# Gates copied out of PSUM by ScalarE, and a state-space branch that is issued later, in a two-layer hybrid attention kernel

## The chip, the cores and the metric

The kernel runs on one core of a Trainium2 chip. Its engines are TensorE (PE in the rows, its weight loads PEld), VectorE (DVE), ScalarE (ACT), GpSimd (POOL) and SyncE (SP, which here only issues transfers). Time is device microseconds (us) of one execution; the number that counts is the median of the runs.

## The reference

Two layers; each normalises x (1024 tokens by 1024 features), makes one wide projection, and feeds three mixers whose outputs are multiplied by SiLU gates and go through one output projection.

```
h = rms_norm(x, norm_g[l]);  proj = h @ w_in[l]
(qa, ka, va, iq, ik, iw, ga, u, gb, cq, ckv, kpe, gc) = split(proj)
ya = dsa_branch(...)     # A: an indexer scores all keys, the top 256 of each query are attended to
yb = s5_branch(u, ...)   # B: complex diagonal state space, scan over time, GELU, GLU
yc = mla_branch(...)     # C: latent attention
mixed = concat(ya * silu(ga), yb * silu(gb), yc * silu(gc))
x = x + mixed @ w_out[l]
```

All is float32. Of branch B three parts count here: a static part (tables and small matrices from the parameters alone), the states (inputs times a matrix, then a complex scan over 128 steps of 8 tokens), and the outputs (states times a matrix, GELU, GLU).

## The kernel before, in words

**Matmuls.** A float32 product is made of three reduced-precision ones (`mm3`, L163 to L165): high by high, low by high, and high by the low part of the weights. So a block of weights is loaded (`raw`), its high part `whi` is written by ACT (L150) and its low part `wlo` by POOL or DVE (L151). PE can't start a block before `whi`, and can't do its third product before `wlo`.

**Stages of a layer.** First the narrow projections and the indexer; then the indexer's scores (PE L927, ACT `rl` L928, DVE sums L933); then the selection of the top keys on DVE (search, then marks L1028 to L1031, whose last instruction writes `bias`, one 128-query block after another; a branch L1040 follows it for a rare case). While DVE selects, PE makes the steps written in `STEPS = "L5C6Q7U01234"`: three projections L, C, Q, the eight gates 0 to 7 of 128 features each, and U, the inputs of branch B. Then the attention items run, block 7 of branch A first: its scores (PE L1394 and L1395), their masked maximum on DVE (L1210, which needs `bias`), exponentials on ACT (L1218), transposes of the exponentials on PE (L1238). Then the output projection.

**Gates.** `gates(c)` makes two halves of 512 tokens, 24 matmuls each, into a PSUM bank `gt`. ACT writes th = tanh(gt/2) (L1164), and DVE writes gate = (th+1)*gt (L1165), reading `th` and the bank. The bank comes free when both have read it. `th` lies in a ring of five 2 KB pieces that other work shares (`s5bd`, `s5rho`, `gl` and more). The gate goes to DRAM and is read back late.

**PSUM** has eight banks: six in one ring (tag `s`: gates, scores, branch B's sums), two for transposes (tag `tr`).

**Branch B** is a generator that the code steps along on a clock of its own: each matmul group of the main line adds its ticks, and each `yield d` of branch B says after how many ticks (times `S5M` = 1.5) it goes on. `static` makes tables (POOL and DVE products L276), small transposed matrices (PE L421 and L438, copied by ACT as `s5k` L423 and `s5w` L439) and rotors `s5R` on POOL (L261 to L266). `chunks` makes the states: sums `vr`, `vi` on PE, products and scans on DVE (L475 to L486), rotation back on POOL (`s5x`, L276). Its last `yield ST2` sets how long after that the `outputs` are written: PE L504 to L506, GELU on ACT and DVE (L509 to L513), transposes L520. It is done for two halves of the groups, 0 and 1. The layer's parameters are prepared by another generator, `params`.

**Order.** A scheduler gives each engine its instructions as one list, worked out before the run, from what each needs and a priority that grows along the program. `side(gen, delay, behind)` starts such a generator after `delay` ticks; `behind` is added to the priority of everything that it issues. In the run each engine goes through its list in order, and waits where the next instruction's inputs, bank or page are not ready.

Of the kernel before, what the change touches and what calls it, by code (L numbers as in the profile page):

```python
# [14 lines left out]
AF = mybir.ActivationFunctionType  # L15
ALU = mybir.AluOpType
# [26 lines left out]
K2 = 5  # L43
MIXT = 4.0
MIX4 = 32
S5P = 0
KVP = -400
TH = (0, 0, 0, 0, 0, 0, 4, 4)
STEPS = "L5C6Q7U01234"
S5W = (0, 0)  # L50
S5M = 1.5
FT = 0.6
ST2 = 8.0
ST3 = 4.0
GLP = 0
KTP = (0, 0, 0)
# [30 lines left out]
def hybrid_kernel(ctx, tc, A, out, dbg=None, layers=DEPTH):  # L87
    nc = tc.nc
    V, S, G, T = nc.vector, nc.scalar, nc.gpsimd, nc.tensor
# [9 lines left out]
    def page(shape, dt, name):  # L99
        return pg.tile(shape, dt, tag="pg", name=name)  # L100
# [4 lines left out]
    def ps_s(shape, name="s"):  # L105
        return pp.tile(shape, F32, tag="s", name=name, bufs=BANKS)
# [12 lines left out]
    def scr(shape, dt, name):  # L119

        n = int(np.prod(shape[1:])) * (2 if dt == BF16 else 4)
        if n > 2048:
            return page(shape, dt, name)
        tag, bufs = ("k1", K1) if n <= 1024 else ("k2", K2)
        return sm.tile(shape, dt, tag=tag, name=name, bufs=bufs)
# [254 lines left out]
    def s5(l, Z, us, yb):  # L380
# [77 lines left out]
        def chunks(gh):  # L458
# [4 lines left out]
            for i in range(4):  # L463
                for e in range(2):
                    rs = slice(64 * e, 64 * e + 64)
                    for x, d in ((0, vr), (1, vi)):
# [24 lines left out]
                                  RR[:, :, j0], RI[:, :, j0], xa[:, :, j0], xb[:, :, j0])  # L491
            yield ST2

# [72 lines left out]
    def side(gen, delay=0.0, behind=0):  # L566

        sides.append([gen, clock[0] + delay, behind])
# [127 lines left out]
    for t in range(8):  # L696
# [3 lines left out]
        if t == 3:  # L700
# [3 lines left out]
            params = s5_params()  # L704
# [10 lines left out]
    for l in range(layers):  # L715
# [16 lines left out]
        def proj_halves(evac):  # L732
            w = [ws.get(), ws.get()]
            for hf in range(2):
                if hf:
                    for _ in turn_h(1, hT, htok, g_in):
                        pass
                pss = [ps_s([128, 2, 256], "pj") for _ in range(2)]
                for kh in range(2):
                    hi, lo, n = w[kh]  # L740
                    for p in range(2):
                        proj_step(pss[p], 4 * hf + 2 * p, kh, hi, lo, n)
                        if kh == 1:
                            evac(2 * hf + p, pss[p])
# [387 lines left out]
        def channels():  # L1132

            hi, lo, _ = ws.get()
            for hf in range(2):
                cs = slice(512 * hf, 512 * hf + 512)
                ps = ps_s([128, 512], "gt")
                for k in range(8):
                    mm3(ps, hi[:, k, :], lo[:, k, :], h_hi[k][:, cs], h_lo[k][:, cs], k == 0, k == 7)
                    tick(0.64)  # L1140
                yield hf, cs, ps
# [18 lines left out]
        def gates(c):  # L1160
            g = page([128, 1024], F32, f"gate{c}")
            for hf, cs, ps in channels():
                th = scr([128, 512], F32, "th")
                S.activation(th, ps, AF.Tanh, scale=0.5)  # L1164
                V.scalar_tensor_tensor(g[:, cs], th, 1.0, ps, op0=ALU.add, op1=ALU.mult)  # L1165
            nc.sync.dma_start(gate_d[c], g)

        yb = []
# [2 lines left out]
        def tables_then_s5():  # L1171
            yield from s5_tables(l, Z)
            for d in s5(l, Z, us, yb):
                yield S5M * d
            for o in range(2):
                gate_in(3 + o)
                (G if GLP else V).tensor_tensor(mixf[3 + o], yb[o], mixf[3 + o], op=ALU.mult)
                mixed.add(3 + o)
        if l == 0:
            side(params, 1.0)  # L1180
        proj_halves(ev_g2)
        proj(ev_iq, tps=range(1, 4), outer="I" not in INNER)

# [279 lines left out]
        def at(i):  # L1463
            if i == S5AT:
                side(tables_then_s5(), behind=S5P)
            if i == CQAT:
# [5 lines left out]
        for i, x in enumerate(STEPS, 8 - len(STEPS)):  # L1472
            at(i)
            if i in QAT:
                next(its)
            if x.isdigit():
                gates(int(x))
            elif x == "U":
                inputs_s5()
            else:  # L1480
                proj(dict(L=ev_g4, C=ev_g3, Q=ev_g5)[x], outer=x not in INNER)
# [56 lines left out]
        for hf in range(2):  # L1538
            cs = slice(512 * hf, 512 * hf + 512)
# [4 lines left out]
        for g in range(2):  # L1544
# [9 lines left out]
            for t in range(8):  # L1554
                cs = slice(128 * t, 128 * t + 128)
                ps = ps_s([128, 512], "po")
# [87 lines left out]
```

## Time and profile before

| | before |
|---|---|
| median of 3 runs | 1354.73 us (1354.72 to 1354.92) |
| profiled execution | 1345.04 us, of which the span shown in the trace is 1343.3 us |
| mean granted TensorE clock over the span | 0.967 of 2.4 GHz |
| PE busy | 1254.7 us, 93% |
| DVE, ACT, POOL busy | 907.3, 662.5, 680.8 us |

The profile is of one execution, 9.7 us shorter than the median of the timed runs; differences are worked out in it and then taken from the median. An engine that is 93% busy need not lose only the other 7%: it is also slower wherever its granted clock falls.

### The profile page before, as it was taken

To read this page: it belongs to the slowest core of one execution; us is meant where nothing else is said; L and a number is where in the kernel's file an instruction comes from. 1 tells how busy PE (TensorE), PEld (TensorE's weight loads), DVE (VectorE), ACT (ScalarE), POOL (GpSimd) and SP (SyncE) were. 2 spreads that over 40 slices of the span, in tenths; PEclk is the share of its full clock that TensorE was granted. 3 is DMA by queue.
4 is the path that set the end of the run, shared out by engine and by line. 5 is a ranking of instruction groups with operands and counts; after the bars stand their busy time and mean duration, and the time that the engine had idled before them with its cause. 6 is when DMAs were issued, how large, how long until landed. Compare 5 with 4: busy or idle time off the path is not lost. (4 is left out here: it accounts for less than half of the span.)

```text
span 1343.3 us, 23872 instructions
## 1 busy us (share of the span) xinstructions
PE 1254.7 (93%) x8644; PEld 1065.8 (79%) x8644; DVE 907.3 (68%) x2430; ACT 662.5 (49%) x1505; POOL 680.8 (51%) x1109
## 2 busy tenths in 40 slices
PE   4898999978999999999999989998889999999998
PEld 4896998757788778877899878977668786887787
DVE  5758889974786797741253878999566778775121
ACT  4346831121778777751243666112148786877300
POOL 3889259766431456312347953795770335553210
PEclk9998999888999999999999989999879999999999
DMA  7200241332110100241140013222303010004202
GB/s 219 72 2 28 83 127 59 96 96 91 39 62 17 42 27 8 76 175 41 79 130 29 20 60 111 82 88 81 121 19 94 8 58 17 12 32 159 78 32 94
DMA packets 78490, 92.78 MB, mean 69 GB/s; under 512 B 13536, under 2 KB 61280, under 8 KB 78368
## 3 DMA queue, kind: packets, MB, share of 16 engines
q1 hardware_dynamic: 77216, 87.03, 20.1%
q0 software_dynamic: 1152, 4.19, 1.0%
q8 instruction: 68, 1.11, 0.3%
q14 instruction: 54, 0.44, 0.1%
HBM read 63.53 MB, written 26.50 MB: 67 GB/s over the span
## 5 line engine op out<-in xcount | busy, mean ns | idle before, releaser
L753 PE MATMUL pj<-whi,hh 128*128 128x256 f32 (+1 forms) x608 | 173.5, 286 | 0.0
L756 PE MATMUL pj<-whi,hl 128*128 128x256 f32 (+1 forms) x608 | 172.3, 285 | 0.0
L755 PE MATMUL pj<-wlo,hh 128*128 128x256 f32 (+1 forms) x608 | 172.1, 283 | 0.0
L151 POOL TENSOR_TENSOR wlo<-raw,whi 128x1024 fp32r<-128x1024 f32 (+1 forms) x40 | 94.3, 2372 | 129.1 <-ACT whi L150 116.5
L163 PE MATMUL gt<-hh,whi 128*128 128x512 f32 x320 | 132.2, 413 | 10.4 <-DVE gate L1165 10.4
L165 PE MATMUL gt<-hh,wlo 128*128 128x512 f32 x320 | 130.7, 409 | 4.1 <-POOL wlo L151 4.1
L164 PE MATMUL gt<-hl,whi 128*128 128x512 f32 x320 | 130.3, 407 | 0.0
L753 PEld LDWEIGHTS pj<-whi,hh 128*128 128x128 f32 x608 | 117.9, 194 | 1.1 <-issue 0.2
L755 PEld LDWEIGHTS pj<-wlo,hh 128*128 128x128 f32 x608 | 117.7, 194 | 0.8
L756 PEld LDWEIGHTS pj<-whi,hl 128*128 128x128 f32 x608 | 117.2, 193 | 0.3
L1244 ACT ACTIVATE pt<-s 128x512 f32<-128x512 f32 (+1 forms) x154 | 82.9, 555 | 47.5 <-PE s L1238 38.2
L933 DVE SCALAR_TENSOR_TENSOR acc<-rl,iw,acc 128x384 f32<-128x384 f32 (+5 forms) x84 | 94.0, 1120 | 13.7 <-ACT rl L928 10.9
L163 PE MATMUL po<-whi,mix 128*128 128x512 f32 x256 | 98.5, 392 | 1.6 <-DVE gin L1261 1.6
L164 PE MATMUL po<-wlo,mix 128*128 128x512 f32 x256 | 99.8, 391 | 0.0
L165 PE MATMUL po<-whi,mix 128*128 128x512 f32 x256 | 99.5, 389 | 0.0
L150 ACT ACTIVATE whi<-raw 128x1024 fp32r<-128x1024 f32 (+1 forms) x54 | 55.9, 1055 | 85.3 <-DMA qa_d<-qo 30.6
L1238 PE MATMUL s<-ident,P 128*128 128x128 f32 x588 | 93.1, 277 | 1.5 <-ACT pt L1244 0.7
L1561 DVE TENSOR_TENSOR xn<-xn,po 128x512 f32<-128x512 f32 x32 | 22.0, 687 | 103.3 <-PE po L165 103.2
L1218 ACT ACTIVATE P<-P,nb,qsc 128x1024 f32<-128x1024 f32 (+7 forms) x96 | 82.4, 864 | 17.0 <-DVE nb L1216 17.0
L1218 ACT ACTIVATE P<-P,nb,asum 128x1024 f32<-128x1024 f32 (+7 forms) x96 | 82.6, 866 | 12.5 <-DVE nb L1216 11.8
L928 ACT ACTIVATE rl<-s 128x512 f32<-128x512 f32 (+3 forms) x160 | 74.0, 540 | 24.4 <-PE s L927 16.6
L1208 DVE TENSOR_SCALAR_CACHE_REDUCE P<-s 128x512 f32<-128x512 f32 (+3 forms) x144 | 74.2, 548 | 16.5 <-PE s L1372 9.9
(453 smaller groups left out, 3625.3 us busy)
## 6 DMA issues: line engine op xcount, KB each, us to landing
raw<-in_w_in SPq DMA_DIRECT2D x32, 512.0 KB, 4.9
gate_d<-gate SPq DMA_DIRECT2D x16, 512.0 KB, 2.9
gin<-gate_d SPq DMA_DIRECT2D x16, 512.0 KB, 4.4
raw<-in_w_out SPq DMA_DIRECT2D x16, 512.0 KB, 6.9
x<-in_x SPq DMA_DIRECT2D x8, 512.0 KB, 4.9
cq_d<-cqs SPq DMA_DIRECT2D x16, 256.0 KB, 2.1
cqT<-cq_d POOLq DMA_DIRECT2D x8, 512.0 KB, 6.0
xn<-in_x SPq DMA_DIRECT2D x8, 512.0 KB, 10.1
```

The lines of the kernel that those rows point to most:

```text
L151: (eng or G).tensor_tensor(lo, raw, f(hi), op=ALU.subtract)
L163: T.matmul(ps, lh, rh, start=start, stop=False)
L164: T.matmul(ps, lh, rl, start=False, stop=False)
L165: T.matmul(ps, ll, rh, start=False, stop=stop)
L753: T.matmul(o, hk, hi[:, k, 0:n], start=kh == 0 and i == 0 and k == 0, stop=False, skip_group_check=True)
L755: T.matmul(o, hk, lo[:, k, 0:n], start=False, stop=False, skip_group_check=True)
L756: T.matmul(o, lk, hi[:, k, 0:n], start=False, stop=kh == 1 and k == 3, skip_group_check=True)
L933: V.scalar_tensor_tensor(a, r[:, 0:nk], w, a, op0=ALU.mult, op1=ALU.add, **({"accum_out": ssum[:, b - 2:b - 1]} if h == 7 else {}))
L1208: V.tensor_scalar(Ps[j][:, c0:c1], p[:, 0:c1 - c0], 1.0, -3.0e38, op0=ALU.mult, op1=ALU.max, accum_out=m)
L1218: S.activation(Ps[j][:, 0:nk], Ps[j][:, 0:nk], AF.Exp, bias=nb[:, j:j + 1], scale=it["scale"][:, j:j + 1], accum_out=sums[:, j:j + 1])
L1238: T.transpose(p[:, i, :], Ps[j][:, 128 * kt:128 * kt + 128], ident)
L1244: S.activation(pt[:, 0:n, :], p[:, 0:n, :], AF.Copy)
```

## The change

Four edits. (1) ACT also copies the bank of a gate into the gate's own page, right after its tanh in the program, and DVE's product then reads `th` and that page, both in SBUF; 32 more ACT instructions of 128 by 512 in all, and a bank of a gate is read by ACT alone. (2) Branch B's whole chain is issued with 700 added to its priority (`S5P`). (3) `ST2` goes from 8 to 24, so its outputs are written 36 ticks after its states and not 12. (4) In layer 0 the parameters of branch B start 12 ticks later and not 1.

```diff
-S5P = 0
+S5P = 700
-ST2 = 8.0
+ST2 = 24.0
@@ gates(c)
                 S.activation(th, ps, AF.Tanh, scale=0.5)
-                V.scalar_tensor_tensor(g[:, cs], th, 1.0, ps, op0=ALU.add, op1=ALU.mult)
+                S.activation(g[:, cs], ps, AF.Copy)
+                V.scalar_tensor_tensor(g[:, cs], th, 1.0, g[:, cs], op0=ALU.add, op1=ALU.mult)
@@
         if l == 0:
-            side(params, 1.0)
+            side(params, 12.0)
```

The lines of the changed kernel behind L1164 have numbers higher by one: L1165 is the copy, L1166 the product, L1211 the masked maximum. What the four edits do to the lists of the engines is alike in both layers; the rows are of layer 0.

On DVE, at the end of the selection, the list before is this (`tkw` is a working copy of a block's scores, `m` eight found values of it, `bias` the mask that the last block's marks become; the rare case behind the branch is left out):

```order
L1029 COPY_PREDICATED m_3187<-kp,consts 128x8
L1030 MATCH_REPLACE tkw<-m_3187,tkw 128x1024
L1031 TENSOR_SCALAR bias<-tkw 128x1024
L1040 COMPARE_AND_BRANCH
...
L1165 SCALAR_TENSOR_TENSOR gate_3156<-th,gt 128x512 x2
L1165 SCALAR_TENSOR_TENSOR gate_3251<-th,gt 128x512 x2
L475 TENSOR_TENSOR s5tab<-vr,s5R 128x512
```

In the list of the changed kernel the first of the two gates (the one numbered 3156 before, 3164 now) stands ahead of the last mark:

```order
L1028 MAX m_3195<-tkw 128x8
L1166 SCALAR_TENSOR_TENSOR gate_3164<-th,gate_3164 128x512 x2
L1029 COPY_PREDICATED m_3195<-kp,consts 128x8
L1030 MATCH_REPLACE tkw<-m_3195,tkw 128x1024
L1031 TENSOR_SCALAR bias<-tkw 128x1024
L1040 COMPARE_AND_BRANCH
...
L1166 SCALAR_TENSOR_TENSOR gate_3261<-th,gate_3261 128x512 x2
L475 TENSOR_TENSOR s5tab<-vr,s5R 128x512
```

Two products have moved ahead of the mark and the branch, and none of them reads a bank any more.

On PE, where the gates end and the attention begins, the list before goes from the last gate matmul over four score pairs (`ka_hi`, `ka_lo` are the two parts of the keys) to branch B's outputs (`s5m`, `s5o` are its small matrices), 24 rows of L504 to L506 in all:

```order
L165 MATMUL gt<-hh_222,wlo 128x512
L504 MATMUL s<-s5m,s5U 128x8x16
L1394 MATMUL s<-ka_hi,qA 128x512
L1395 MATMUL s<-ka_lo,qA 128x512
...
L504 MATMUL s<-s5m,s5U 128x8x16
L505 MATMUL s<-s5o,s5x 128x8x16 x2
L506 MATMUL s<-s5o,s5x 128x8x16
L504 MATMUL s<-s5m,s5U 128x8x16
```

In the changed kernel all twelve score pairs of the first three items stand ahead of the outputs, of which 12 rows come there and the other 12 among the later attention work:

```order
L1395 MATMUL s<-ka_hi,qA 128x512
L1396 MATMUL s<-ka_lo,qA 128x512
L504 MATMUL s<-s5m,s5U 128x8x16
L505 MATMUL s<-s5o,s5x 128x8x16
L1395 MATMUL s<-ka_hi,qA 128x512
L1396 MATMUL s<-ka_lo,qA 128x512
L506 MATMUL s<-s5o,s5x 128x8x16
L504 MATMUL s<-s5m,s5U 128x8x16
...
L506 MATMUL s<-s5o,s5x 128x8x16
L1239 MATMUL tr<-ident,P 128x128
```

So the scores went ahead, half of the outputs and their eight transposes went behind the first transposes of the exponentials. The second half of branch B goes much further back, from the first quarter of the attention to its middle. DVE's list follows: its twelve maxima L1210 stood behind the GELU L510 to L513 of the outputs, and now stand right behind the scan L486.

On ACT, the tanh, copies and weight parts of the gates before, and the copies `s5k`, `s5w` of branch B between them:

```order
L1164 ACTIVATE th<-gt 128x512
L150 ACTIVATE whi<-raw 128x1024
L1164 ACTIVATE th<-gt 128x512
L423 ACTIVATE s5k<-tr 16x512 x2
L1164 ACTIVATE th<-gt 128x512
L439 ACTIVATE s5w<-tr 128x512
L1164 ACTIVATE th<-gt 128x512
L439 ACTIVATE s5w<-tr 128x512
```

The same stretch of the changed kernel:

```order
L150 ACTIVATE whi<-raw 128x1024
L1164 ACTIVATE th<-gt 128x512 x2
L423 ACTIVATE s5k<-tr 16x512
L1165 ACTIVATE gate_2996<-gt 128x512 x2
L423 ACTIVATE s5k<-tr 16x512
L439 ACTIVATE s5w<-tr 128x512
L1164 ACTIVATE th<-gt 128x512 x2
L473 ACTIVATE s5rho<-zp 128x512
L439 ACTIVATE s5w<-tr 128x512
L150 ACTIVATE whi<-raw 128x1024
L1165 ACTIVATE gate_3164<-gt 128x512 x2
```

The copies don't always follow their tanh: here they stand behind branch B's copies, and so behind what those wait for.

## Rows read from the trace of the kernel before

**Rows 1.** The page, busy time, share of the span and instructions by engine.

```profile
PE 1254.7 (93%) x8644; PEld 1065.8 (79%) x8644; DVE 907.3 (68%) x2430; ACT 662.5 (49%) x1505; POOL 680.8 (51%) x1109
```

**Rows 2.** Stretches: length, busy PE, PEld, DVE, ACT, POOL (instructions), clock, DMA.

```profile
258.90:343.10 84.20, 70.48 (x321) 55.81 (x321) 56.03 (x105) 21.60 (x35) 52.52 (x105) 0.84 0.26 85
913.60:996.90 83.30, 68.50 (x323) 53.94 (x321) 55.47 (x103) 21.37 (x34) 52.36 (x107) 0.86 0.26 86
```

**Rows 3.** Waits of PE in layer 0's stretch: total us, times, longest.

```profile
PE gt L163 <- DVE gate L1165: 4.4, 1, 4.4
PE pb L1035 <- ACT s5w L439: 3.4, 1, 3.4
PE s L506 <- POOL s5x L276: 3.4, 1, 3.4
```

**Rows 4.** Waits of PE in layer 1's stretch, the longest.

```profile
PE gt L163 <- DVE gate L1165: 5.9, 1, 5.9
```

**Rows 5.** Timeline of DVE, layer 0: start, duration, instruction, idle before and its releaser.

```profile
288.27 2.06 DVE L1031 TENSOR_SCALAR bias<-tkw 128x1024 bf16<-128x1024 f32 x1
291.28 2.48 DVE L1165 SCALAR_TENSOR_TENSOR gate<-th,gt 128x512 f32<-128x512 f32 x4 [0.96 <-DVEq L1040]
...
329.41 0.60 DVE L510 TENSOR_SCALAR gl<-gl 128x512 f32<-128x512 f32 x1 [12.02 <-ACT gl L509]
...
332.11 0.68 DVE L1210 CUSTOM_DVE_ANT_0 P<-s,bias 128x512 f32<-128x512 f32 x1
...
344.00 0.69 DVE L1210 CUSTOM_DVE_ANT_0 P<-s,bias 128x512 f32<-128x512 f32 x1
```

**Rows 6.** Branch B's outputs on PE: half 0 of layer 0, then half 1.

```profile
322.40:334.30 11.90, 11.90 (x41) 8.98 (x41) 4.09 (x10) 1.23 (x2) 7.75 (x17) 0.51 0.08 23
412.20:416.40 4.20, 4.20 (x27) 3.23 (x25) 2.58 (x11) 2.67 (x7) 1.30 (x1) 1.00 0.00 0
```

**Rows 7.** Groups of instructions: count, busy us, mean ns, idle before.

```profile
L1165 DVE SCALAR_TENSOR_TENSOR gate<-th,gt 128x512 f32<-128x512 f32 x32 | 21.0, 682 | 8.1 <-ACT th L1164 5.3 <-DVEq L1040 1.8 <-DMA qa_d<-qo 0.7
L1244 ACT ACTIVATE pt<-s 128x512 f32<-128x512 f32 (+1 forms) x154 | 82.9, 555 | 47.5 <-PE s L1238 38.2 <-PE acc_o L1231 7.7 <-PE s L1395 0.5
```

**Rows 8.** Timeline, products of two SBUF operands on DVE, and of POOL beside the first.

```profile
254.66 3.85 DVE L276 TENSOR_TENSOR s5tab<-zp 128x512 f32<-128x512 f32 x2
254.04 3.92 POOL L1011 TENSOR_TENSOR tkw<-acc,tkm 128x640 f32<-128x640 f32 x2
305.26 0.69 DVE L478 TENSOR_TENSOR s5z<-s5tab 128x512 f32<-128x512 f32 x1
```

**Rows 9.** Timeline of PE: gate matmuls ahead of the stretch, first transposes of exponentials.

```profile
258.02 0.39 PE L163 MATMUL gt<-hh,whi 128*128 128x512 f32 x1
258.25 0.39 PE L164 MATMUL gt<-hl,whi 128*128 128x512 f32 x1
...
343.09 0.66 PE L1238 MATMUL tr<-ident,P 128*128 128x128 f32 x4 [1.19 <-ACT s5gT L521]
```

**Rows 10.** Timeline of ACT and POOL: weight parts for gates, then `s5x`.

```profile
265.36 1.06 ACT L150 ACTIVATE whi<-raw 128x1024 fp32r<-128x1024 f32 x1 [3.27 <-issue]
266.55 2.40 POOL L151 TENSOR_TENSOR wlo<-raw,whi 128x1024 fp32r<-128x1024 f32 x1 [6.68 <-ACT whi L150]
291.23 1.06 ACT L150 ACTIVATE whi<-raw 128x1024 fp32r<-128x1024 f32 x1 [7.01 <-DVEq L1040]
321.09 1.26 POOL L276 TENSOR_TENSOR s5x<-s5tab 128x508 f32<-128x508 f32 x1
```

**Rows 11.** The attention of layer 0 in 20 us stretches, their sum; one stretch of the selection.

```profile
sum 260.00, PE 251.49 PEld 206.43 DVE 190.34 ACT 197.20 POOL 100.90; mean PE 19.35 PEld 15.88 DVE 14.64 ACT 15.17 POOL 7.76
240.00:260.00 20.00, 17.18 (x70) 13.26 (x68) 19.59 (x29) 1.06 (x1) 18.56 (x19) 0.91 0.27 79
```

**Rows 12.** Waits of PE over the whole span, earlier stages.

```profile
PE s L927 <- ACT rl L928: 8.0, 7, 3.9
PE tr L678 <- DVE hl L682: 6.0, 2, 4.5
```

## The prediction

> **What bounds the kernel now.** I read the page first: PE is busy for 93% of the span and no other engine for more than 68% [rows 1]. So time can be gained where PE waits or runs at the lower clock, and of those places I looked at the ones that the change touches. The view by stretches shows them: from the end of the first gates to the first transposes of exponentials, 84.2 us in layer 0 and 83.3 in layer 1, PE is busy 70.5 and 68.5 us at a granted clock of 0.84 and 0.86 [rows 2]. That is 13.7 and 14.8 us of idle time, and 0.16 x 84.2 = 13.5 and 0.14 x 83.3 = 11.7 us lost to the clock: 27.2 and 26.5 us, the most that any edit of this stretch alone can give. In the attention behind it PE is busy 251.5 of 260 us, at full clock [rows 11].
>
> The waits say who is late. In layer 0: 4.4 us for DVE's gate product, 3.4 for the copy `s5w`, 3.4 for `s5x` [rows 3]; in layer 1 the gate's wait is 5.9 [rows 4]. The timeline of DVE explains the first: the last mark runs from 288.27 to 290.33, then comes the branch, and only then, at 291.28, four gate products that PE's banks had waited for [rows 5]. Behind the gates DVE stands still for 12.0 us (GELU, waiting for branch B's outputs) while score banks are ready, since its maxima L1210 are in line behind the GELU; the first starts at 332.11 and the twelfth at 344.00 [rows 5]. PE meanwhile does branch B's outputs at half clock: 41 instructions in 11.9 us at 0.51 [rows 6].
>
> **The change, part by part.**
>
> *ACT copies.* Nothing in the rows is this instruction; the nearest is ACT's copy of a 128x512 PSUM tile, 0.555 us [rows 7]. 32 of them are 17.8 us, 16 to a layer, on an engine that is busy 21.6 of 84.2 us in the stretch [rows 2]; its room hides them, except where one stands behind something late. Without that cover each would hold its bank 0.56 us longer.
>
> *DVE product.* From bank and `th` it takes 0.682 us [rows 7]. A product of two SBUF operands of the same size takes 0.69 [rows 8], so I price the new form the same. The other bound is in the same rows: two such products took 3.85 us together while POOL ran 3.92 us of large tiles beside them, 1.9 each [rows 8]. The Trainium skill (Perfetto Trace Analysis, Optimizing Scalar/DVE Operations) has an access overhead of about 125 ns for DVE on PSUM and 60 on SBUF, by which 32 products would save an estimated 2.1 us of DVE; the two rows at 0.68 and 0.69 don't show that. The same section says that GpSimd and DVE share an SBUF port, and the 1.9 us rows agree.
>
> *Waits for gate banks* (4.4 and 5.9) go, since no bank waits for DVE. What is late next is the weights, so the gain is not the wait. I followed PE through layer 0. The gate matmuls come 0.23 us apart [rows 9]. PE stands at 258.5; it now makes 16 more, to 262.2, and a few of branch B's small matrices, which I estimate at 1.2 us. The next block needs a `whi` that ends at 266.4, and its third products a `wlo` that ends at 268.95 [rows 10]; both hang on earlier transfers that the change leaves. So some 5 us of waiting are new there. 44 matmuls from 269 last 10.1 us, up to 1.7 more at the lower clock: 279 to 281. Then 1.2 us of small matrices, and a wait for four ACT copies in line (two `s5k`, two gate halves, at 0.56 each [rows 7] 2.2 us): the 3.4 us for `s5w` are only moved. `s5w` and the sums `vr`, `vi` with a short wait of their own, some 3 us, end at about 286.5. Two gates, 96 matmuls, are 22 us, with 1 to 3 us (an estimate) for gate copies that stand behind `vi` and for one more `wlo`: 310 to 312.
>
> *Outputs and scores.* The twelve score pairs are next, paced by twelve maxima of 0.68 us [rows 5], 8.2 us, with the scan and a product or two between: 320 to 325. That is 20 us ahead of before, but PE's next instruction, L506, needs the second `s5x`. It ended at 322.35 [rows 10], and now follows two more POOL products in line: about 325. Twelve output rows, 24 instructions, are 24 x 4.2/27 = 3.7 us at full clock, or 24 x 11.9/41 = 7.0 at the half rate seen [rows 6]. So the first transposes of exponentials come between 327 and 337; I take 331, the lower middle, because PE is fed by the scores until just before. Before they came at 343.1 [rows 9]: 12 us earlier. But 3.7 us of outputs and eight transposes (four are 0.66 us [rows 9], so 1.3) now lie behind, in an attention in which PE is full [rows 11], so their 5.0 us come back. Net 7, bounds 11 and 1; if the scores ran at half clock too, so that the transposes came at 341, -3. Layer 1 has the same lists; its longer gate wait (5.9) is swallowed by the same weights, and I give it the same 7.
>
> *The second half of branch B*, moved to the middle of the attention, has the same instructions. PE has no hole there to lose, and DVE is busy 190 of 260 us [rows 11]: cost 0, bounds -3 and +3 per layer.
>
> *Earlier stages.* PE waits 8.0 us in seven places for ACT's `rl` [rows 12]; pages now come free in another order, and ACT's extra copies stand between some `rl`: 0, bounds -3 and +3 per layer. The late parameters thin DVE's list where layer 0's wait for `hl` is, 4.5 of the 6.0 us [rows 12]: 1 us gained, bounds 0 and 4.5.
>
> Sum: 7 + 7 + 0 + 1 = 15 us. The profiled execution would go from 1345.0 to 1330; it stands 9.7 us under the median, and I take the difference from the median: 1354.7 - 15 = 1340.
>
> **The rivals.**
>
> *The stretch flows.* If ACT's copies keep the banks moving, PE's gaps stay short and the half-clock stretch of the outputs goes too. Of 27 us per layer [rows 2], the new waits for weights (5) and for `s5k` and `s5w` (3), without clock loss, would be left, and the 5 us of moved work: 27 - 8 - 5 = 14 per layer, 28 in all, with the prologue 29: 1326. For it: the outputs' half clock followed waits that DVE's order made. Against: the weights' gaps are of the same size as those before which the clock fell.
>
> *It doesn't do what it says.* PE is off DVE, but on ACT, which goes through its list in order, with copies behind branch B's copies and `vi`. If these hold the banks as long as DVE did, and `s5x` and the clock hold the outputs at 337 or later, the 6 us gained are the 5 given back: 1 us per layer, 1352 to 1355. For it: every stall of [rows 3] has a successor in my working.
>
> *Slower, through DVE's operands.* Gate products now read SBUF twice, while in the selection POOL is busy 18.6 of 20 us and DVE 19.6 [rows 11]. If the eight products ahead of the last mark all took 1.9 us for 0.68 [rows 8], that is 9.8 us, and the two that are now in line ahead of the mark are 1.4: the mark would end not at 290.3 but at 301.5. The `whi` of the last gate waits for the branch behind the mark; it began at 291.23 before [rows 10], would begin at 302.4, and the two weight parts take 1.06 and 2.40: 305.9. PE comes to the last gate 48 matmuls before 310 to 312, so at 299 to 301. So up to some 5 us of delay cost nothing, and from there each counts once: here 5 to 6 us, with 3 more at the lower clock, against the 7; with the second half of branch B at its bound, 3, that is a loss of 5 per layer and, less the 1 us of the early stage, 1364. The last mark's delay is the shared port's price in this kernel, whose rule is the one named above. Against it: POOL's large tiles are there for some of the products only, and the rows show 0.69 where it rests.
>
> **How the numbers follow.** Forecast (gain of 4 to 25 us, by the bounds 1 and 11 of a layer, those of the earlier stages, and a share of the clock): 0.57. Flows: 0.13. No change: 0.13. Slower: 0.17, as the moved work and DVE's operands both have unknown prices. A measurement of this kernel tells 0.2%, 2.7 us, from no change. Faster is then 0.57 + 0.13 = 0.70, same 0.13, slower 0.17. The forecast's own range is 1330 to 1351. The range for 8 in 10 takes in most of the flowing case and the near part of the slower one: 1320 to 1359.
>
> **What would show it.** Right: no wait of a gate matmul on DVE; waits of about 3 us and 2.5 for `whi` and `wlo` behind 262; the first L1211 at 312 to 316 and the twelfth by 326; first transposes near 331; a gain that stands at 12 us there and shrinks by about 5 through the attention. Wrong: gate products over 1 us on DVE and a last mark behind 298; a half-clock stretch of 10 us or more still at the outputs or at the scores; a gain that is larger at the end of the attention than at its start; or a loss in the indexer's scores, where I put nothing.

## The result, and the profile after

The changed kernel takes 1370.29 us (median of 4, 1369.33 to 1377.58) against 1354.82 for the kernel before: 1.0126 of it, 95% interval 1.0091 to 1.0161. It is 15.5 us slower, where 15 us faster was forecast, and lies outside the range.

The profile of [rows 2] was of an execution 9.7 us below the median. So the kernel before was profiled once more (run e12 below); that execution took 1354.11 us, and what follows is measured against it. The lists are the same in both. Of the 9.0 us between the two spans (1343.3 and 1352.3 us) the two gate stretches have 3.8 and 4.6, counted from the end of gate 7: 95.8 and 94.3 us in the first profile, 99.6 and 98.9 in e12. The largest part is one wait of PE. In the first profile it took 2.1 us, just ahead of the stretch of [rows 3]; in e12 it takes 6.4. First its row in the first profile, then PE's wait in e12's stretch of layer 0:

```profile
249.93 0.50 PE L165 MATMUL gt<-hh,wlo 128*128 128x512 f32 x1 [2.05 <-POOL wlo L151]
```

```profile
PE gt L165 <- POOL wlo L151: 7.7, 2, 6.4
```

Stretches of layer 0, then layer 1, in the second profile of the kernel before: from the first indexer scores, from the end of gate 7, from the first transposes of exponentials, and from the point where half of these are done to the output projection. The columns are the length, the busy time (instructions) of PE, PEld, DVE, ACT and POOL, the clock, and the DMA share.

```profile
90.20:247.90 157.70, 151.08 (x915) 133.81 (x914) 143.17 (x283) 72.85 (x167) 104.83 (x138) 0.98 0.23 71
247.90:347.50 99.60, 80.33 (x352) 62.44 (x352) 69.51 (x123) 21.38 (x34) 67.75 (x120) 0.81 0.27 84
347.50:471.80 124.30, 122.72 (x1075) 98.65 (x1076) 92.48 (x322) 96.87 (x235) 37.22 (x68) 0.99 0.15 43
471.80:596.40 124.60, 119.83 (x1024) 100.95 (x1023) 93.72 (x335) 95.72 (x241) 61.63 (x115) 0.99 0.20 68
748.90:907.30 158.40, 151.01 (x915) 133.88 (x913) 142.59 (x283) 72.47 (x167) 105.73 (x139) 0.98 0.23 71
907.30:1006.20 98.90, 78.74 (x353) 61.40 (x353) 70.69 (x123) 21.33 (x34) 67.87 (x119) 0.83 0.27 84
1006.20:1130.30 124.10, 122.40 (x1075) 98.52 (x1076) 92.25 (x322) 96.86 (x235) 36.85 (x68) 0.99 0.15 44
1130.30:1254.80 124.50, 119.81 (x1023) 100.91 (x1024) 93.74 (x335) 95.67 (x241) 61.66 (x115) 0.99 0.20 65
```

The same stretches of the changed kernel:

```profile
91.14:254.70 163.56, 153.67 (x915) 136.55 (x914) 142.85 (x292) 75.55 (x173) 115.69 (x146) 0.96 0.23 72
254.70:340.25 85.55, 71.23 (x323) 55.62 (x321) 67.81 (x118) 22.43 (x39) 55.52 (x81) 0.89 0.28 89
340.25:465.04 124.79, 117.40 (x1040) 95.06 (x1040) 90.03 (x308) 94.17 (x232) 46.85 (x103) 0.97 0.12 36
465.04:608.84 143.80, 138.59 (x1090) 112.31 (x1088) 101.29 (x349) 101.65 (x254) 62.70 (x115) 0.96 0.19 65
761.36:918.81 157.45, 150.72 (x915) 134.00 (x913) 142.57 (x289) 75.46 (x173) 109.59 (x141) 0.98 0.24 74
918.81:1005.02 86.21, 71.45 (x323) 54.19 (x321) 68.81 (x119) 23.54 (x41) 57.11 (x83) 0.89 0.29 90
1005.02:1129.49 124.47, 117.51 (x1040) 95.50 (x1040) 89.26 (x308) 93.09 (x230) 45.68 (x102) 0.97 0.12 36
1129.49:1270.03 140.54, 135.33 (x1089) 109.81 (x1088) 100.72 (x347) 100.93 (x250) 62.32 (x115) 0.99 0.19 64
```

The differences, layer 0 and layer 1:

| stretch | forecast | measured |
|---|---|---|
| indexer and projections | 0 | +5.9, -0.9 |
| gates to first transposes | -12 | -14.1, -12.7 |
| first half of the attention | +5 for both halves | +0.5, +0.4 |
| second half of the attention | | +19.2, +16.0 |

So the first transposes came out about as forecast; against the first profile, from which the forecast was made, they are 10.3 and 8.1 us earlier and not 14.1 and 12.7. The loss is in the attention, 19.7 and 16.4 us for 5, and in layer 0's indexer. Its place is the second half of the attention. The first half is as long as before, though PE has 35 instructions less there and is busy 5 us less. The attention of the kernel before hardly differs between its two profiles: 248.1 and 248.8 us in the first, 248.9 and 248.6 in e12.

PE's waits in layer 0's gate stretch of the changed kernel:

```profile
PE gt L163 <- ACT whi L150: 3.5, 1, 3.5
PE s L1395 <- DVE qA L1391: 3.3, 3, 2.3
PE gt L165 <- POOL wlo L151: 3.0, 1, 3.0
PE tr L438 <- ACT s5k L423: 2.1, 1, 2.1
PE s L506 <- POOL s5x L276: 1.5, 1, 1.5
PE gt L163 <- ACT gate L1165: 0.7, 1, 0.7
```

No gate matmul waits for DVE any more. Of the successors that the prediction named, `whi`, the copies `s5k` (2.1 us, worked out 2.2), a gate copy and `s5x` are there. The `wlo` wait is not the one that it named: it stands at the matmul where e12 waits 6.4 us.

The new instruction on ACT and the product on DVE, all 32 of each:

```profile
L1165 ACT ACTIVATE gate<-gt 128x512 f32<-128x512 f32 x32 | 18.2, 594 | 2.2 <-PE vi L467 2.2
L1166 DVE SCALAR_TENSOR_TENSOR gate<-th,gate 128x512 f32<-128x512 f32 x32 | 31.9, 1011 | 14.8 <-ACT gate L1165 14.7
```

The copy is 0.594 us (0.555 was taken), the product 1.011 and not 0.69.

### The profile page after: what moved, and what is told of

Read it like the earlier page. It is cut to its first block, busy times and chain, and to the rows that moved or that the text cites. A ratio compares the mean times of both kernels' runs of the same rounds, so it can differ in the third digit from the quotient of the medians.

```text
span 1367.6 us, 23861 instructions
## 1 busy us (share of the span) xinstructions
PE 1269.1 (93%) x8644; PEld 1070.5 (78%) x8644; DVE 921.9 (67%) x2430; ACT 675.5 (49%) x1537; POOL 689.2 (50%) x1109
## 5 line engine op out<-in xcount | busy, mean ns | idle before, releaser
L1239 PE MATMUL s<-ident,P 128*128 128x128 f32 x588 | 98.5, 285 | 2.4 <-ACT P L1219 1.7
L165 PE MATMUL po<-whi,mix 128*128 128x512 f32 x256 | 99.6, 390 | 0.0
L164 PE MATMUL po<-wlo,mix 128*128 128x512 f32 x256 | 99.6, 390 | 0.0
L1219 ACT ACTIVATE P<-P,nb,qsc 128x1024 f32<-128x1024 f32 (+7 forms) x96 | 82.5, 870 | 10.6 <-DVE nb L1217 10.6
```

Of the source, the lines that this page charges most:

```text
L164: T.matmul(ps, lh, rl, start=False, stop=False)
L165: T.matmul(ps, ll, rh, start=False, stop=stop)
L1219: S.activation(Ps[j][:, 0:nk], Ps[j][:, 0:nk], AF.Exp, bias=nb[:, j:j + 1], scale=it["scale"][:, j:j + 1], accum_out=sums[:, j:j + 1])
L1239: T.transpose(p[:, i, :], Ps[j][:, 128 * kt:128 * kt + 128], ident)
```

## The experiments

Times are medians. The kernel before was timed beside each of the five sets, on the same chip, and its median lay between 1351.9 and 1355.3 us. The ratios are to it; they are not the quotients of the medians. The traces are of one execution each.

**Each edit alone.** e1 has the copies, e2 `S5P`, e3 `ST2`, e4 the late parameters, each as in the diff above.

> Only the ACT copies of the gates (edit 1), the rest as before. Theory M (the loss of the whole change comes from branch B's work moved into the attention, where it holds PE up; the copies alone help the gates): the waits of gate matmuls on DVE, 10.3 us in both layers, go, some of them to weights, and the end is 3 to 10 us earlier than before, 1345 to 1352. Rival C (the copies are the loss, as ACT's list in order and the two SBUF operands of DVE hold up the indexer and the attention): 8 us or more later than before, 1363 or more.

> Only S5P 0 to 700 (edit 2). Theory M: the second half of branch B goes into the middle of the attention and the end is 10 to 25 us later, 1365 to 1380, with the attention longer in both layers and the gates as before. Rival C: within 4 us of before, 1351 to 1359.

> Only ST2 8 to 24 (edit 3). Theory M: outputs later but branch B's states where they were: the score pairs go ahead of the outputs, PE's half-clock stretch at the outputs gets shorter, and the second half costs little: between 6 us earlier and 4 later, 1349 to 1359. Rival C: the same. If ST2 and not S5P moves the second half's outputs into the attention at a loss, 8 us or more later.

> Only the late parameters (edit 4). Theory M and rival C: within 2 us of before, 1353 to 1357. Rival P (the 7 us that layer 0's indexer lost are the parameters' work, which now stands among the indexer's on DVE and POOL): 5 to 9 us later, all of it in layer 0 ahead of the gates, 1360 to 1364.

Measured: e1 1363.09 us (1.0068, interval 1.0042 to 1.0094), e2 1362.98 (1.0060, 1.0043 to 1.0077), e3 1367.08 (1.0075, 1.0054 to 1.0096), e4 1365.12 (1.0080, 1.0054 to 1.0105). Each edit alone loses 8 to 12 us. Theory M is wrong in two parts: the copies alone don't gain, and it is `ST2`, not `S5P`, that moves the second half of branch B into the middle of the attention. Rival C foresaw e1, but not that the three others lose as much. Rival P foresaw e4 roughly: of its 10 us, 5.2 are lost by the end of layer 0's indexer scores. The first transposes come 14.7 us earlier in e3 than in e12 in layer 0, and the attention is longer by about as much as in the changed kernel, 19.3 and 18.7 us:

```profile
332.80:601.00 268.20, 254.14 (x2127) 204.07 (x2128) 192.93 (x656) 196.96 (x482) 108.17 (x217) 0.98 0.16 52
998.65:1265.98 267.33, 254.09 (x2126) 204.89 (x2127) 192.69 (x657) 196.63 (x483) 108.01 (x217) 0.97 0.16 51
```

Layer 0's gate stretch, split at the last gate matmul, tells what the copies and `ST2` each do there. The rows are of e12, e1 (copies), e3 (`ST2`) and the changed kernel, two each:

```profile
247.86:320.57 72.71, 58.29 (x269) 45.78 (x269) 57.94 (x92) 12.86 (x21) 46.79 (x72) 0.86 0.33 102
320.57:347.52 26.95, 22.08 (x85) 16.69 (x84) 11.64 (x31) 8.53 (x13) 21.02 (x49) 0.68 0.10 35
250.05:316.27 66.22, 55.06 (x270) 43.33 (x268) 53.02 (x77) 16.64 (x29) 42.35 (x67) 0.92 0.31 97
316.27:349.82 33.55, 23.67 (x86) 17.48 (x84) 17.85 (x39) 9.53 (x15) 22.68 (x49) 0.64 0.12 43
248.28:320.61 72.33, 57.88 (x268) 45.57 (x269) 56.69 (x92) 12.85 (x21) 45.17 (x71) 0.86 0.33 102
320.61:332.80 12.19, 10.89 (x55) 8.37 (x53) 11.18 (x31) 3.44 (x7) 11.59 (x15) 0.98 0.18 60
254.68:319.83 65.15, 55.58 (x270) 44.53 (x268) 49.19 (x77) 16.71 (x29) 41.20 (x65) 0.92 0.31 96
319.83:340.26 20.43, 15.68 (x55) 11.11 (x53) 18.64 (x43) 5.73 (x10) 14.35 (x16) 0.77 0.18 66
```

The copies shorten the gates by 6.5 us, and all of it is lost between the gates and the first transposes, where PE waits 5.7 us for `s5x` (3.6 in e12). `ST2` leaves the gates as long as they were, with a wait of 4.5 us for DVE among them, and shortens the way behind them by 14.8, with 30 instructions less there. So `ST2` alone brings the whole gain at the first transposes (84.5 us for 99.7), and the copies add nothing to it (85.6). Layer 1 is alike: 98.9 us in e12, 98.7 in e1, 85.4 in e3, 86.2 in the changed kernel.

**The change without one edit, and two edits together.** e7 is the change with `ST2 = 8.0`, e16 with `side(params, 1.0)`; e8 is the kernel before with the copies and the late parameters.

> The whole change but with ST2 back at 8. Theory H and rival D: the loss between the middle and the three-quarter mark of the attention, 17 to 20 us a layer, goes, and so does the gain of 10 at the first transposes; what stays are the losses of the other three edits, 5 to 9 us a layer: 1363 to 1373. If S5P moves branch B back as far as ST2 does, the loss in the attention stays: 1380 or more.

> The whole change with the parameters as before. The late parameters alone lost 5.2 us at the end of layer 0's indexer and the whole change 7.6: if it is theirs here too, 3 to 7 us earlier than the whole change, 1363 to 1368, all of it in layer 0 ahead of the gates. If it comes from the copies or from chance in the order: 1369 to 1373.

> The ACT copies and the late parameters, without S5P and ST2. If the two losses are costs of the edits themselves (the copies hold ACT up, the parameters stand in the indexer), they add: 8 and 10 us, 1371 to 1375. If they come from the order that the scheduler finds after any edit (PE's list around branch B is here again as in the kernel before, unlike in each edit alone), less than either: 1355 to 1363.

Measured: e7 1366.92 us (1.0121, 1.0071 to 1.0170), e16 1364.05 (1.0075, 1.0045 to 1.0105), e8 1362.19 (1.0054, 1.0038 to 1.0071). e7: the loss of the attention and the gain at the first transposes go together, as expected (gate stretches of 100.6 and 99.4 us, attentions of 249.0 and 252.3). It still costs almost what the whole change costs: 7.4 us are lost by the end of layer 0's indexer scores and 3.7 in layer 1's attention. e8: the two losses don't add, so part of each seems to be the order that an edit brings and not the edit. e16 is 6.2 us less than the whole change, and its trace says where: at the end of layer 0's indexer scores it stands 0.9 us behind e12, and the whole change 7.6. PE's waits in that stretch, first of the changed kernel, then of e16:

```profile
PE tr L880 <- POOL iqr L180: 3.8, 2, 1.9
PE s L927 <- ACT rl L928: 3.0, 4, 2.3
PE s L927 <- DVE iqs L884: 2.2, 1, 2.2
```

```profile
PE s L927 <- ACT rl L928: 2.4, 3, 1.8
PE s L927 <- DVE ck L1068: 2.3, 1, 2.3
```

The indexer's queries (`iqr` by POOL, `iqs` by DVE) are 6 us of waiting in the one, and absent from the other. So the late parameters cost 5 to 7 us in layer 0's indexer: 5.2 alone, 6.7 in the whole change.

**What PE's work is worth in either half of the attention.** The second half of branch B's outputs and its GLU stand in the first half of the attention in the kernel before, in the second half with `ST2` at 24. e5 (before) and e6 (`ST2` 24) issue those outputs twice; e9 and e10 leave a part out:

```diff
+                    for _ in range(1 + gh):            # e5, e6: twice for the second half
                     T.matmul(p[:, :, i, :], U[:, g, :], M[:, g, :], ...)
                     T.matmul(p[:, :, i, :], X[rs, 0, pl, :], Wf[rs, 0, pl], ...)
                     T.matmul(p[:, :, i, :], X[rs, 1, pl, :], Wf[rs, 1, pl], ...)
```

```diff
-                    T.matmul(p[:, :, i, :], U[:, g, :], M[:, g, :], start=True, stop=False)
+                    T.matmul(p[:, :, i, :], U[:, g, :], M[:, g, :], start=True, stop=gh == 1)
+                    if gh == 0:                        # e9, e10: the second half without its states
                         T.matmul(p[:, :, i, :], X[rs, 0, pl, :], Wf[rs, 0, pl], ...)
                         T.matmul(p[:, :, i, :], X[rs, 1, pl, :], Wf[rs, 1, pl], ...)
...
-                for k in range(2):
+                for k in range(1):                     # GLU: half of the inputs
```

> The kernel before, but the output matmuls of branch B's second half (24 rows a layer, L504 to L506) are issued twice, at the place where they stand, about a third into the attention; their result is unchanged. They take 4.2 us for 12 rows, so this adds 8.4 us of PE work a layer. Theory H (the first half of the attention is paced by ACT and DVE, and branch B's matmuls filled PE's holes there for nothing): 0 to 6 us later than before in all, 1355 to 1361, none of it seen at the output projection beyond 3 us a layer. Rival D (PE's work costs the same wherever it stands, and the moved chain does harm by the waits that it makes on DVE): 14 to 18 us later, 1369 to 1373.

> The same doubling in the kernel with ST2 at 24 alone, where these matmuls stand in the second half of the attention. Theory H: 8.4 us a layer, 14 to 18 us later than the kernel with ST2 at 24, 1381 to 1385. Rival D: the same 14 to 18. The two differ by what the early doubling costs.

> The kernel before without a part of branch B's work on PE: the second half's outputs leave out the two state terms (L505, L506, 32 instructions a layer at 0.16 us) and the GLU half of its inputs (8 instructions at 0.43), 8.5 us of PE work a layer, a third into the attention. Theory B (balance: in the first half of the attention ACT and DVE need as long as PE with branch B's work in it, so more PE work costs its full time, less gives little back): 0 to 8 us earlier than before in all, PE idle for the rest. Rival D (PE's work costs the same wherever it stands): 14 to 18 us earlier, 1337 to 1341.

> The same work left out of the kernel with ST2 at 24 alone, where it stands in the second half of the attention. Theory B and rival D: 8.5 us a layer, 14 to 18 us earlier than that kernel, 1349 to 1353 by its median of 1367. If the second half of the attention has room too: 0 to 8 us earlier, 1359 to 1367.

Measured: e5 1377.96 us (1.0179, 1.0162 to 1.0196), e6 1382.01 (1.0196, 1.0171 to 1.0220), e9 1347.35 (0.9975, 0.9953 to 0.9997), e10 1346.80 (0.9954, 0.9933 to 0.9976). More work early costs 23 us for 17, so theory H, that there is room, fell; that it costs more than its own time no run explains. Less work early gives 4.5 us of 17, so rival D fell too. Late, both go at about the full price: by the medians e6 is 15 us over e3 and e10 is 20 under it, by the ratios both are 16 from it. That left theory B: in the kernel before, PE is just full in the first half of the attention, and without a part of its work something else holds the stretch at nearly the same length. The expectation took ACT and DVE for this; no run shows what it is, and they are busy 191 and 184 of 242 us in e9's layer 0. The traces agree on the length. The attention of e9, layer 0 and layer 1:

```profile
347.68:589.97 242.29, 234.29 (x2057) 194.54 (x2058) 183.67 (x656) 191.39 (x475) 100.00 (x182) 0.98 0.18 57
999.43:1247.95 248.52, 236.08 (x2058) 195.68 (x2058) 188.00 (x657) 192.75 (x478) 98.20 (x182) 0.97 0.17 54
```

It is 6.6 and 0.1 us shorter than in e12 (248.9 and 248.6), for 8.5 us of work each; in layer 1 PE has 12.4 us without work there instead of 6.4.

e17 (before) and e18 (`ST2` 24) put the same extra PE work, spread evenly, into the first half of the attention: every second group of transposes of exponentials is issued twice (`nt` counts the groups).

```diff
+                nt[0] += 1
-                for i, (j, kt) in enumerate(bl):
+                for i, (j, kt) in list(enumerate(bl)) * (1 + (18 <= nt[0] < 54 and nt[0] % 2)):
                     T.transpose(p[:, i, :], Ps[j][:, 128 * kt:128 * kt + 128], ident)
```

> The kernel before with 72 transposes of exponentials a layer issued twice, every second group of four in the first half of the attention (7.6 us a layer at 0.106 us each); the result is unchanged. Theory B (in the kernel before PE has no room there, since branch B's second half fills it): 13 to 20 us later than before, 1366 to 1374. If PE has room there in any case: 0 to 6 us.

> The same 72 transposes in the kernel with ST2 at 24 alone, where branch B's second half has gone from that stretch and left waits of 8.7 us for 2.5 between the first transposes and the middle. Theory B: they fall into the room that it left, 0 to 6 us later in both layers than that kernel's 1367, 1364 to 1373. Rival G (the stretch isn't paced by ACT and DVE; the waits are those of the moved chain, at places of its own): 13 to 18 us later, 1380 to 1385.

Measured: e17 1369.87 us (1.0093, 1.0071 to 1.0115), e18 1372.04 (1.0124, 1.0106 to 1.0142). The attention of e17, then of e18:

```profile
349.41:605.51 256.10, 249.13 (x2168) 207.32 (x2168) 185.28 (x657) 193.27 (x474) 98.19 (x181) 0.99 0.17 52
1015.34:1271.67 256.33, 250.76 (x2168) 208.52 (x2168) 185.16 (x657) 193.53 (x474) 97.54 (x181) 0.98 0.16 52
```

```profile
335.78:605.68 269.90, 258.52 (x2196) 211.69 (x2197) 193.02 (x657) 197.18 (x483) 108.65 (x217) 0.98 0.17 52
1001.64:1271.53 269.89, 258.65 (x2198) 211.64 (x2198) 193.03 (x657) 197.00 (x481) 108.58 (x217) 0.98 0.16 50
```

The same 7.6 us a layer cost 7.2 and 7.7 us where branch B's second half fills PE (248.9 and 248.6 without them), and 1.7 and 2.6 where it has gone (268.2 and 267.3). This is what shows theory B: moving the second half away left 5 to 6 us of room a layer that nothing filled, and the same work has its full price where PE is full. An edit that moves nothing there can shift a layer's attention by some us as well (e8: 247.4 and 254.9), but here both layers say the same.

**The second half put back, and tries at a better kernel.** e11 is the kernel before with only this; e13 the whole change with it; e14 the kernel before with it and with copies for gates 0 to 4; e15 the kernel before with those copies alone.

```diff
-            yield ST2
+            yield 16.0 if gh == 0 else 0.5
...
+                if c < 5:                              # e14, e15
+                    S.activation(g[:, cs], ps, AF.Copy)
-                V.scalar_tensor_tensor(g[:, cs], th, 1.0, ps, ...)
+                V.scalar_tensor_tensor(g[:, cs], th, 1.0, g[:, cs] if c < 5 else ps, ...)
```

> The kernel before with ST2 at 16 for the first half of branch B and 0.5 for the second: on PE the first half's outputs then stand behind 16 to 24 score matmuls, as with ST2 at 24, and the second half's outputs and GLU where they stood before, at about the same score and transpose of the attention. Theory B: the 10 us gained at the first transposes stay, less the 4 to 5 us of outputs that now lie behind them: 5 to 12 us earlier than before in both layers together, 1343 to 1350. Rival E (any new order costs some 8 to 10 us against the one of before, as each single edit did): 1358 to 1366.

> The kernel before once more, for a second profile of it, since the first was of an execution 9.7 us below the median. Its lists are the same, so waits for other engines should be the same to some tenths, and a longer time should show as lower granted clock: if it comes at about 1355, the span is 9 to 11 us longer, with 10 us or more of it in stretches at 0.5.

> The whole change, but ST2 16 for the first half of branch B and 0.5 for the second, so that the second half's outputs and GLU stand a third into the attention again. Theory B (the moved second half is the loss: 14.7 and 11.3 us beyond the moved first-half rows, by the two traces): most of 26 us comes back, 1344 to 1352, at or under the kernel before; the first transposes stay 10 us or more earlier in both layers. Rival F (the attention loses by the copies, the priority or chance, wherever the second half stands): 1362 or more.

> ACT's copies for gates 0 to 4 alone (those ahead of the attention; gates 5 to 7 stand beside the indexer), ST2 16 and 0.5 as above, no S5P, parameters as before. Theory B: the indexer as before, the gates' gain of 8 us a layer and that of the outputs behind the scores, 5 us of moved rows to pay: 6 to 16 us earlier than before, 1338 to 1348. Rival E (any new order costs 8 to 10): 1355 to 1365.

> ACT's copies for gates 0 to 4 alone and nothing else. If the copies of gates 5 to 7 cost layer 0's indexer its 2.9 us, that goes against the kernel with all copies (1363): 1357 to 1361, still later than before, as the gates' gain of 6 to 7 us is lost at branch B's outputs, whose place is as before and which wait for the same s5x. If the copies themselves are the loss in the attention: 1363.

Measured: e11 1352.83 us (1.0007, 0.9986 to 1.0028), e13 1371.03 (1.0131, 1.0095 to 1.0167), e14 1361.46 (1.0057, 1.0025 to 1.0089), e15 1369.44 (1.0124, 1.0091 to 1.0157). None beats the kernel before. e12 was expected to have the same waits to some tenths, and its `wlo` wait is 4.4 us longer. e11 came out between the ranges of theory B and rival E: it keeps 8.2 and 6.6 us of the gain in the gate stretch (91.4 and 92.3 us) and gives 10.1 and 5.3 back in the attention. Still, with the second half of branch B at its place it has 1.0007 where e3 has 1.0075. As 12 output rows of the first half also stand earlier than in e3, ahead of the first transposes, the pair is no test of the second half alone. The attention of e11:

```profile
340.83:599.80 258.97, 251.52 (x2104) 206.15 (x2103) 184.48 (x653) 191.60 (x470) 108.08 (x214) 0.96 0.17 54
1003.24:1257.18 253.94, 246.18 (x2104) 201.35 (x2103) 184.97 (x653) 191.50 (x470) 108.81 (x214) 0.98 0.18 55
```

e13 fell against theory B's expectation and came out where rival F has it, and e14 where rival E has it; e15 is above all that was named for it. The attention of e13:

```profile
351.57:611.04 259.47, 248.68 (x2104) 201.03 (x2103) 183.44 (x651) 192.05 (x471) 106.21 (x214) 0.98 0.16 52
1012.91:1273.91 261.00, 250.37 (x2104) 202.91 (x2103) 184.01 (x651) 192.27 (x471) 105.88 (x214) 0.97 0.16 50
```

It is 9.1 and 4.0 us shorter than in the changed kernel, but the gate stretch is longer by 9.8 and 5.5 (95.3 and 91.7 us), as all 24 output rows stand ahead of the first transposes again. And 10.6 and 12.4 us over e12 remain in an attention that has hardly more instructions (2104 for 2098). One wait there is new, 2.9 us of PE for DVE's `gin` product in layer 0; the rest is spread, and no run took it apart. e15 shows that the copies of gates 5 to 7 are not what cost e1 its 2.9 us by the end of layer 0's indexer scores: without them it is 2.5.

## Why the prediction was wrong

*The gates (steps "Waits for gate banks" and "Outputs and scores"): right in path and about right in size, wrong in what the copies are worth.* Forecast 12 us raw in each layer, measured 14.1 and 12.7 against e12, 10.3 and 8.1 against the first profile; PE's waits are the ones that were named, but for `wlo`. The gain is that of `ST2`: e3 has all of it without the copies, and e1, with the copies alone, none. Of the misses in date, 7.4 us are what layer 0 had lost before. The first transposes came at 340.3 for 331, so 1.9 later beyond that; the first L1211 began at 326.5 and the twelfth at 336.1, for 312 to 316 and 326, so 3 to 7 and 2.7 later beyond that.

*The step that failed* is "*The second half of branch B*, moved to the middle of the attention ... PE has no hole there to lose ... cost 0, bounds -3 and +3 per layer". The rows said that PE was full in the attention [rows 11]; it doesn't follow that the time falls when work is taken out. The first half of the attention, without the second half of branch B, stayed at its length (+0.5 and +0.4 us), and the second half, with it, grew by 19.2 and 16.0. By e17 and e18 the room left behind is 5 to 6 us of the 7.6 tried; by e9 three quarters of the work left out early give nothing back; e11, with the second half at its place, is 9 us faster than e3. So the step put at nothing what has a price. That it makes up the whole of 19.7 and 16.4 us isn't shown: in the whole change the move back (e13) returns 9.1 and 4.0 us of the attention, and the gate stretch takes as much.

What the attention's 19.7 us of layer 0 are made of can be estimated from the stretches: 24 output instructions and eight transposes more, some 5 us (forecast 5.0); PE without work for 12.6 us instead of 6.4, so 6.2; and the clock, 0.03 x 124.8 + 0.04 x 143.8 = 9.5 us lost against 0.01 x 248.9 = 2.5, so 7.0, give or take 2 as the rows give the clock to hundredths. These are some 18 of 19.7. So the loss beyond the 5 us shows partly as waits and partly as clock. From the end of gate 7 to the output projection the two layers came out at +5.6 and +3.7 us, for -7 and -7. (The 27 us that the prediction gives as the most that the gate stretch can return count a wait at the lower clock twice, as idle time and as clock.)

*The parameters* were forecast to gain 1 us, bounds 0 and 4.5. They lose 5 to 7, a stage later than where the wait was looked at (`hl`, whose longest wait of PE went from 4.5 us to 4.1): the indexer's queries come late. The bound 0 excluded a loss without a reason. A loss in the indexer's scores was among the signs of being wrong.

*The DVE product* was taken at its lower bound, 0.69; it took 1.01 on average, 10.9 us more in all. This is the price that the rival "slower" was made of. The Trainium skill (Perfetto Trace Analysis, Optimizing Scalar/DVE Operations) says that GpSimd and DVE share an SBUF port, and the trace agrees: 2.5 us beside POOL's `wlo`, below. The sign named for it came, products over 1 us and a last mark behind 298 (it began at 300.9, with the 7.4 us in it). But the rival's place was wrong: the product that took 2.5 us stands behind the mark, no wait of PE for the last gate's weights went over the 3.5 us named, and the gate stretch gained as forecast. So slower came out, at +15 and not by that mechanism.

*The edits don't add.* The four alone lose 8.3, 8.2, 12.3 and 10.3 us, the whole change 15.5. That part of each loss is the new order of lists that any edit brings is argued from this, from e8 and from e14, and not shown by a run of its own. The prediction priced instructions and moves, and had no term for that.

*Left open:* why the attention loses 10.6 and 12.4 us with the second half put back (e13). e11 loses about the same in layer 0, 10.1, without the copies, the priority and the late parameters, so there these aren't needed for it; some 8 of its 10.1 us are clock, 0.96 for 0.99 over 259 us. In layer 1 it loses 5.3. Open too is what of the single edits' losses is order by chance, and what holds the first half of the attention at its length when PE has less to do.

## What to carry to other kernels

Where an engine is full because a side branch fills its gaps, as PE here, that branch can be nearly free at its place (4.5 us of 17) and cost its full time elsewhere (16 of 17 by the ratios). Before moving it, leave part of it out once, and add as much: if both cost the full time, the engine is the bound there; if leaving out gives little, the stretch has a second limit just below. When two edits go in together, try each alone where the forecast adds them up: here the copies' gain at the gates was gone before the first transposes. And profile the kernel before twice when a forecast rests on a stretch: here two executions differed by 3.8 and 4.6 us in the two stretches that were priced.

## What the runs showed of the hardware that was not expected

DVE's product of two SBUF operands waited for a POOL tile as if locked out. In the changed kernel, with the product's two halves from 306.53 (the first took 2.51 us) and POOL's `wlo`:

```profile
306.09 2.40 POOL L151 TENSOR_TENSOR wlo<-raw,whi 128x1024 fp32r<-128x1024 f32 x1 [2.45 <-ACT whi L150]
...
306.53 3.21 DVE L1166 SCALAR_TENSOR_TENSOR gate<-th,gate 128x512 f32<-128x512 f32 x2 [4.86 <-ACT gate L1165]
```

This first half ended 0.55 us after POOL's instruction. In the kernel before, with one operand in PSUM, the second and third of three halves ran beside the same POOL instruction:

```profile
291.88 1.88 DVE L1165 SCALAR_TENSOR_TENSOR gate<-th,gt 128x512 f32<-128x512 f32 x3
...
292.36 2.38 POOL L151 TENSOR_TENSOR wlo<-raw,whi 128x1024 fp32r<-128x1024 f32 x1 [0.33 <-ACT whi L150]
```

They took 0.63 us each: an operand in PSUM kept the product out of POOL's way. All 32 products, shortest, median and longest in ns, in e12 and in the changed kernel:

```profile
L1165 DVE SCALAR_TENSOR_TENSOR gate<-th,gt x32: 674/681/689, 129.5 to 981.1; 128x512 f32<-128x512 f32 x32
L1166 DVE SCALAR_TENSOR_TENSOR gate<-th,gate x32: 665/717/2507, 133.6 to 990.8; 128x512 f32<-128x512 f32 x32
```

And the kernel before itself lay between 1343.3 and 1357.5 us over the runs here, while its first four agreed within 0.2 us.
